# A decoder trunk on one core: the loads of the output projections spread between other projections' steps

## The chip, the core and the metric

The kernel runs on one core of one Trainium2 chip. Its time is the device time of one execution in microseconds (us); less is better. TensorE (PE) multiplies, ScalarE (ACT), VectorE (DVE) and GpSimd (POOL) do the elementwise work, SyncE (SP) issues every DMA used here.

## The reference

Two decoder layers over 1024 tokens of width 1024, and a final norm, all float32:

```python
# layer 0
z = rms_norm(x, g_in) @ w_in        # q/kv latents, rope key, sliding-window q/k/v, gate
o = concat(latent_attention(z), sliding_window_attention(z))   # 8 heads each
x = x + (o * silu(gate)) @ w_out
# layer 1
z = rms_norm(x, g_in) @ w_in        # q, k, v, forget logits, gate
o = forgetting_attention(z)         # 16 heads, causal, decay bias
x = x + (o * silu(gate)) @ w_out
out = rms_norm(x, g_final)
```

## The kernel before

Every matrix product is done in three TensorE passes on split operands: a float32 value is cast to a high part on ACT, and the low part is the difference (`split`, `split_sb`; lines 104, 105, 112, 113). `mm3` (lines 116 to 118) issues high times high, high times low and low times high.

**Attention.** A unit is one head and one half of the queries. It makes rows of logits into PSUM (lines 116 to 118 or 268, 269), DVE takes the running minimum (line 322), ACT the exponential (line 329), POOL scales the row (line 284). Then TensorE transposes the row, 128 columns at a time, into PSUM (line 355), ACT and DVE split it into `ph` and `pl` (lines 104, 105), and TensorE multiplies with the values (lines 346, 347). PSUM has two banks each for logits (`s`), transposes (`t`), values (`o`) and projections (`pj`).

**Order on TensorE.** It is written out by hand. `run_units` reads a string for each unit: T is a transpose group, L a row of logits, M a value product, F one step of other work. F calls `fill.step()`, which takes the next step of the first entry of `fill.work`, if all that this entry waits for is done. An entry is a projection that the current heads don't need yet (16 steps: 8 for each half of the tokens), or one token block of an output projection (4 steps). Each step is three or six matmuls on 512 columns. `fill.loads` is a second list, taken in order as soon as an entry is free, without counting steps. Where the work of a layer's list is left after its last unit, `fill.drain()` issues it back to back.

**Order on the other engines.** ACT, DVE, POOL and SP are ordered by a scheduler, from its own estimate of when operands are ready and a buffer is free. So a load or a cast can stand in its engine's queue well ahead of its place in the program.

**The output projections.** Layer 0's is done in two parts: `swa_out` (line 1004) for the sliding-window heads, 8 blocks for each half `q` of the output columns, with weights from `swa_wo(q)` (line 995, four pieces of 128x512 into `kx` tiles); and `out0` (line 1126) for the latent heads, with weights from `load_wo` (line 1063, eight pieces into the `hh`, `hl` tiles that held the normed input). Layer 1's is `out1_first` and `out1` (lines 1288 and 1295), with sixteen pieces from `load_wo`. A block of gated heads (`ogs`) is read back from memory into a `wr` tile and split into `wh` and `wl` at the start of the block's own first step (`swa_out`, `out_parts`). There are 5 `wr` tiles and 3 each of `wh` and `wl`; the weights of every projection pass through the same tiles.

**When the weights are loaded before.** All four pieces of `swa_wo(0)` in one entry of `fill.loads`; all four of `swa_wo(1)` at the end of block 7 of the first half; all eight pieces of layer 0's second part in one entry of `fill.loads`, after the last gate projection; eight pieces of layer 1 when the first half of gate 6 is written, and two more in each of the next four blocks.

Of the kernel before, what the change touches and what calls it, by code (L numbers as in the profile page):

```python
# [13 lines left out]
F32R = mybir.dt.float32r  # L14
# [5 lines left out]
P = 128  # L20
# [41 lines left out]
def trunk(ctx, tc, x, positions, e_g_in, e_w_in, e_g_q_a, e_w_q_up, e_g_kv_a, e_w_kv_up,  # L62
# [47 lines left out]

    def split_sb(hi, lo, raw, engine=None):
        nc.scalar.copy(out=hi, in_=raw)  # L112
        (engine or nc.gpsimd).tensor_tensor(out=lo, in0=raw, in1=hi.bitcast(F32), op=ALU.subtract)  # L113
# [310 lines left out]
    class Filler:  # L424


        def __init__(self):
            self.work, self.loads, self.done = [], [], set()

        def add(self, name, gen, after=()):  # L430
# [3 lines left out]
        def load(self, name, gen, after=()):  # L434
            self.loads.append((name, gen, after))

        def free(self, items):
            return items and all(a in self.done for a in items[0][2])

# [8 lines left out]
        def step(self):  # L448
            self.ahead()
            if self.free(self.work):  # L450
                try:
                    next(self.work[0][1])
                except StopIteration:
                    self.done.add(self.work.pop(0)[0])
                    self.step()

        def need(self, *names, ready=None):
            for name in names:
                while name not in self.done and not (ready and ready()):
                    self.ahead()  # L460
                    if name not in self.done:
                        assert self.free(self.work), (name, self.work[0], self.loads[:1])
                        self.step()

        def drain(self):
            while self.work or self.loads:
                self.ahead()
                assert self.free(self.work) or not self.work, self.work[0]
                self.step()

    fill = Filler()
# [532 lines left out]
    def swa_out(q, blk):  # L1004
# [6 lines left out]
        nc.sync.dma_start(out=r, in_=x[tok, cols])  # L1011
        acc = pst("pj")
# [10 lines left out]
    def first_wo():  # L1023
        swa_wo(0)
        yield

    units = []
# [8 lines left out]
    for h in range(8):  # L1036
        fill.load(f"prep{h}", mla_prep(h, heads[h]),
                  [[("rows", "swa", 5, 1)], [("rows", "swa", 7, 1), ("pv", "swa", 6, 1)],
                   [("rows", "mla", 0, 1), ("pv", "swa", 7, 1)]][h] if h < 3 else
                  [("rows", "mla", h - 2, 1), ("pv", "mla", h - 3, 1)])  # L1040
        if h == 1:
            fill.load("wp", first_wo(), [("rows", "swa", 7, 1)])
    for pr in range(4):
        for d, G in UNIT_ORDER[pr == 3]:
            units.append(mla_unit(2 * pr + d, G))
    for w in WORK0.split():
        kind, i = w[0], int(w[1])
        if kind == "q":
            fill.add(f"qs{i}", swa_q(i), [("rows", "swa", 2 * i - 3, 1)] * (i > 1))
        elif kind == "s":  # L1050
            fill.add(f"sgate{i}", gate_chunk(swa_gate(i), hT, None, ogs0[i]), [("pv", "swa", 2 * i + 1, 1)])
        elif kind == "p":
            q, blks = ((0, range(NB)), (1, range(4)), (1, range(4, NB)))[i]
            for blk in blks:
                fill.add(f"p{q}{blk}", swa_out(q, blk), ["wp", "sgate3", ("pv", "swa", 7, 1)])
# [7 lines left out]
    def load_wo(w, e0, halves):  # L1063

        n = KC - e0
        for nh in range(2):
            if nh * n % KC == 0:
# [10 lines left out]
    def out_parts(blk, ogs, own, e0s):  # L1078

        tok = slice(blk * P, (blk + 1) * P)  # L1080
        parts = []
        for e0 in e0s:
            raw = sbt("wr", [4, P])
            oh, ol = sbt("wh", [4, P], F32R), sbt("wl", [4, P], F32R)
            n = 4 if e0 == 0 else 3
            nc.sync.dma_start(out=raw[:, 0:n, :], in_=ogs[e0:e0 + n, :, tok].rearrange("e p t -> p e t"))
            split_sb(oh[:, 0:n, :], ol[:, 0:n, :], raw[:, 0:n, :])
            if e0:
# [3 lines left out]

    def out_proj(nh, blk, parts, wo, resid, dst=None, e0=0, part=slice(0, 512)):

# [6 lines left out]
        for e, og in enumerate(parts):  # L1101
            mm3(acc, *og, wh[:, e0 + e, part], wl[:, e0 + e, part], e == 0, e == len(parts) - 1)
            if e < len(parts) - 1:
                yield
        nc.vector.tensor_tensor(out=r if dst is None else dst, in0=acc, in1=r, op=ALU.add)
        if dst is None:
# [19 lines left out]
    def out0(nh, blk):  # L1126
        if nh == 0:
            xa.append(sbt(("qh", "ql", "kh", "kl")[blk] if blk < 4 else "r1", [D]))
        half = xa[blk][:, nh * 512:(nh + 1) * 512]
        yield from out_proj(nh, blk, out_parts(blk, ogs0, pairs[3]["ot"], [4]), wo, xps, half)  # L1130
        square_sum(half, ssqs[nh][blk // 4][:, blk % 4:blk % 4 + 1])
# [113 lines left out]
    wo1_parts = []  # L1245
    wo1_load = load_wo(wo1, 0, wo1_parts)

    def fox_gate(pr, halves=(0, 1)):
        evac = gate_evac(fox[pr]["gt"])

        def and_load(hf, acc):
            evac(hf, acc)
            if (pr, hf) == (6, 0):
                for _ in range(KC):
                    next(wo1_load)
        return project([(w1, FG + pr * P, FG + (pr + 1) * P)], hT, and_load, halves)

# [28 lines left out]
    fill.load("gfin", final_gain(), [("rows", "fox", 13, 1)])  # L1286

    def out1_first(nh, blk):
        parts = out_parts(blk, ogs1, None, [0])
        for _ in range(KC // len(FIRST)):  # L1290
            next(wo1_load, None)
        yield from out_proj(nh, blk, parts, wo1_parts, x1s)
        yield

    def out1(blk):
        y = [sbt("r0", [512]) for _ in range(2)]
        e0s = [4] if blk in FIRST else [0, 4]
        parts = out_parts(blk, ogs1, fox[7]["ot"], e0s)
        pieces = [(0, 0, 512), (1, 0, 512)] if blk < NB - 1 else [(0, 0, 512), (1, 0, 256), (1, 256, 512)]
        total = None  # L1300
        for nh, a, b in pieces:
            cols = y[nh][:, a:b]
            yield from out_proj(nh, blk, parts, wo1_parts, x1s, cols, e0s[0], slice(a, b))
            ss = sbt("sm", [1])
# [9 lines left out]
        for nh in range(2):  # L1314
# [4 lines left out]
            nc.sync.dma_start(out=out[blk * P:(blk + 1) * P, nh * 512:(nh + 1) * 512], in_=y[nh])  # L1319

    for nh in range(2):
        for blk in FIRST:
            fill.add(f"first{nh}{blk}", out1_first(nh, blk))
    for blk in range(NB):
        fill.add(f"out1{blk}", out1(blk), ["gfin", ("pv", "fox", 15, blk // 4)])
    with tc.manual_schedule(engines={mybir.EngineType.PE}):
# [23 lines left out]
```

## Time and profile before

| | us |
|---|---|
| median of 3 runs | 1194.89 (1194.58 to 1195.39) |
| the profiled execution | 1195.06 |
| its span, first to last instruction | 1193.3 |
| TensorE busy in the span | 1168.4 (98%) |
| VectorE, ScalarE, GpSimd busy | 726.3, 702.5, 594.1 |

A busy share is an average over stages; a matmul's end in the profile is modelled, so a matmul that starts late can still look back to back with the one before. A stretch of idle time in front of an instruction stands in brackets with what ended it.

### The profile page before, as it was taken

The numbers are of one execution on the slowest core, as the hardware profiler recorded it, in microseconds if no ns is written. First come the engines' busy times: TensorE is split into PE (matmuls) and PEld (weight loads), VectorE is DVE, ScalarE is ACT, GpSimd is POOL, SyncE is SP. The second block draws the span as 40 slices with busy tenths as digits, with TensorE's granted clock in tenths as the row PEclk, the third lists the DMA queues.
The fourth block names the chain that finished last, engine by engine and source line by source line (L and its number), as shares of the span: only waits on it lengthen the run. The fifth ranks groups of instructions, "written<-read, shape, count | busy, mean of one in ns | idle before, by whom it ended". The sixth has DMA issues, their size and how long they took to land. (4 is left out here: it accounts for less than half of the span.)

```text
span 1193.3 us, 20029 instructions
## 1 busy us (share of the span) xinstructions
PE 1168.4 (98%) x6600; PEld 1001.9 (84%) x6600; DVE 726.3 (61%) x1921; ACT 702.5 (59%) x1585; POOL 594.1 (50%) x741
## 2 busy tenths in 40 slices
PE   9999999999999999999999999999999999999997
PEld 6898788888888877889998888888888888877886
DVE  6673466677777776663004666666666666667754
ACT  5445477776776665555115667676767675766532
POOL 6421154565655565335005556656555555568452
PEclk9999999999999999999999999999999999999999
DMA  6326522454653452654213222313222323147441
GB/s 202 96 63 229 159 46 62 125 150 133 164 164 106 135 155 89 201 175 135 85 56 100 62 72 62 89 57 95 61 81 71 84 59 106 63 130 230 164 157 62
DMA packets 157086, 135.30 MB, mean 113 GB/s; under 512 B 53259, under 2 KB 121638, under 8 KB 156982
## 3 DMA queue, kind: packets, MB, share of 16 engines
q1 hardware_dynamic: 156982, 134.02, 37.3%
q8 instruction: 52, 0.85, 0.3%
q14 instruction: 52, 0.43, 0.1%
HBM read 96.43 MB, written 37.55 MB: 112 GB/s over the span
## 5 line engine op out<-in xcount | busy, mean ns | idle before, releaser
L116 PE MATMUL pj<-hh,wh 128*128 128x512 f32 (+1 forms) x792 | 320.3, 404 | 0.0
L118 PE MATMUL pj<-hh,wl 128*128 128x512 f32 (+1 forms) x792 | 308.8, 390 | 0.6 <-POOL wl L113 0.6
L117 PE MATMUL pj<-hl,wh 128*128 128x512 f32 (+1 forms) x792 | 308.6, 390 | 0.0
L113 POOL TENSOR_TENSOR wl<-wr,wh 128x512 fp32r<-128x512 f32 (+1 forms) x130 | 163.7, 1262 | 137.9 <-ACT wh L112 121.3
L284 POOL TENSOR_SCALAR r<-r,sm 128x256 f32<-128x256 f32 (+4 forms) x250 | 170.8, 692 | 121.4 <-DVE sm L331 68.1
L105 DVE TENSOR_TENSOR pl<-t,ph 128x512 fp32r<-128x512 f32 (+1 forms) x320 | 178.8, 564 | 84.7 <-ACT ph L104 82.5
L104 ACT CAST ph<-t 128x512 fp32r<-128x512 f32 (+1 forms) x320 | 153.8, 484 | 110.5 <-PE t L355 92.5
L118 PEld LDWEIGHTS pj<-hh,wl 128*128 128x128 f32 x792 | 148.7, 188 | 33.4 <-POOL wl L113 1.0
L329 ACT ACTIVATE r<-r,sm 128x128 f32<-128x128 f32 (+7 forms) x184 | 143.1, 778 | 55.5 <-DVE sm L322 53.6
L116 PEld LDWEIGHTS pj<-hh,wh 128*128 128x128 f32 x792 | 149.1, 188 | 22.0 <-ACT r L891 0.4
L117 PEld LDWEIGHTS pj<-hl,wh 128*128 128x128 f32 x792 | 149.5, 189 | 20.5
L355 PE MATMUL t<-ident,r 128*128 128x128 f32 x828 | 135.6, 273 | 6.4 <-DVE pl L105 4.6
L355 PEld LDWEIGHTS t<-ident,r 128*128 128x128 f32 x828 | 103.5, 140 | 34.5 <-DVE pl L105 6.0
L112 ACT CAST wh<-wr 128x512 fp32r<-128x512 f32 (+1 forms) x130 | 77.7, 599 | 54.6 <-PE pj L117 23.9
L316 POOL TENSOR_TENSOR ld<-ld,zrow 128x128 f32<-128x128 f32 x128 | 57.9, 463 | 100.2 <-DVE sm L322 78.6
L346 PE MATMUL o<-ph,v 128*128 128x512 f32 (+3 forms) x288 | 106.9, 371 | 0.0
L347 PE MATMUL o<-pl,v 128*128 128x512 f32 (+3 forms) x288 | 99.4, 346 | 0.0
L322 DVE CUSTOM_DVE_ANT_0 r<-s,ld 128x512 f32<-128x512 f32 (+1 forms) x120 | 67.6, 563 | 47.2 <-PE s L269 44.1
L293 POOL TENSOR_TENSOR v<-ge,v 128x512 fp32r<-128x512 f32 x26 | 34.6, 1331 | 91.9 <-ACT v L292 91.9
L346 PEld LDWEIGHTS o<-ph,v 128*128 128x128 f32 x288 | 54.4, 189 | 7.7
L347 PEld LDWEIGHTS o<-pl,v 128*128 128x128 f32 x288 | 54.6, 190 | 6.2
L276 DVE TENSOR_TENSOR og<-o,ob 64x512 f32<-64x512 f32 x64 | 43.9, 686 | 10.7 <-ACT ob L275 9.7
(337 smaller groups left out, 2432.7 us busy)
## 6 DMA issues: line engine op xcount, KB each, us to landing
wr<-in_o_w_in SPq DMA_DIRECT2D x62, 256.0 KB, 3.2
ld<-lcs SPq DMA_DIRECT2D x16, 512.0 KB, 3.9
ogs<-og SPq DMA_DIRECT2D x28, 256.0 KB, 2.0
wr<-ogs SPq DMA_DIRECT2D x28, 256.0 KB, 3.6
ge<-vscr SPq DMA_DIRECT2D x24, 256.0 KB, 3.2
gt<-x1s SPq DMA_DIRECT2D x23, 256.0 KB, 2.8
wr<-ogs SPq DMA_DIRECT2D x24, 192.0 KB, 3.2
wr<-in_e_w_in SPq DMA_DIRECT2D x16, 256.0 KB, 3.3
```

The source lines that it names most:

```text
L104: nc.scalar.copy(out=hi, in_=src)
L105: nc.vector.tensor_tensor(out=lo, in0=src, in1=hi.bitcast(F32), op=ALU.subtract)
L112: nc.scalar.copy(out=hi, in_=raw)
L113: (engine or nc.gpsimd).tensor_tensor(out=lo, in0=raw, in1=hi.bitcast(F32), op=ALU.subtract)
L116: nc.tensor.matmul(out=o, lhsT=ah, rhs=bh, start=first, stop=False)
L117: nc.tensor.matmul(out=o, lhsT=ah, rhs=bl, start=False, stop=False)
L118: nc.tensor.matmul(out=o, lhsT=al, rhs=bh, start=False, stop=last)
L284: nc.gpsimd.tensor_scalar(out=row, in0=row, scalar1=rc, scalar2=scale, op0=ALU.mult, op1=ALU.mult)
L329: nc.scalar.activation(out=row[:, 0:L], in_=row[:, 0:L], func=AF.Exp, scale=-1.0, bias=mn, accum_out=den)
L346: nc.tensor.matmul(out=O[0][:, cols], lhsT=v()[:, j, :], rhs=ph[:, cols], start=j == 0, stop=False)
L347: nc.tensor.matmul(out=O[0][:, cols], lhsT=v()[:, j, :], rhs=pl[:, cols], start=False, stop=j == n - 1)
L355: nc.tensor.transpose(out=t[:, b * P:(b + 1) * P], in_=rows[b][:, j * P:(j + 1) * P], identity=ident)
```

## The change

Four things are changed, and no arithmetic.

1. `Filler` gets a third list, `sides`: an entry advances by one piece at every `every`-th step of other work that is taken while the entry is free (4 for `swa_wo`, 2 for `load_wo`). `unblock` advances it at once where the first entry of `work` waits for nothing but that side entry.
2. `swa_wo` and `load_wo` give up control after each piece. The piece's DMA is issued in one advance, and its cast and subtraction in the next; the cast is held in ACT's queue behind what the program put there before it (`keep_in_program_order`).
3. The eight pieces of layer 0's second part may begin when the first half of gate 3 is written, and a block of `out0` waits only for the four pieces that it uses. Layer 1's sixteen pieces become two entries, free when the first half of gate 6 is written and after gate 7.
4. The gated heads of a block are read and split during the second step of the block before it (`more`, `out_load`, `swa_load`), where there is one in the same list.

```diff
-    def split_sb(hi, lo, raw, engine=None):
-        nc.scalar.copy(out=hi, in_=raw)
+    def split_sb(hi, lo, raw, engine=None, in_order=False):
+        cast = nc.scalar.copy(out=hi, in_=raw)
+        if in_order:
+            tc.keep_in_program_order(cast)
...
+        def side(self, name, gen, every, after=()):
+
+            self.sides.append((name, gen, after, every))
+
+        def missing(self, items):
+            return [a for a in items[0][2] if not (a() if callable(a) else a in self.done)]
...
+        def advance(self):
+
+            if next(self.sides[0][1], self) is self:
+                self.done.add(self.sides.pop(0)[0])
+
+        def unblock(self):
+
+            while self.work and self.free(self.sides):
+                rest = self.missing(self.work)
+                if not rest or any((a[0] if type(a) is tuple else a) != self.sides[0][0] for a in rest):
+                    break
+                self.advance()
...
         def step(self):
             self.ahead()
+            self.unblock()
             if self.free(self.work):
+                if self.free(self.sides):
+                    self.ticks += 1
+                    if self.ticks % self.sides[0][3] == 0:
+                        self.advance()
...
     def swa_wo(q):
+        late = None
...
-            split_sb(wh, wl, raw)
+            if late:
+                late()
+            late = partial(split_sb, wh, wl, raw, None, True)
+            yield
+        late()
+        yield
...
+    def swa_out(q, blk, more=None):
+
+        tok, cols = slice(blk * P, (blk + 1) * P), slice(512 * q, 512 * (q + 1))
+        oh, ol, r = ahead.pop(("swa", q, blk), None) or swa_load(q, blk)
         acc = pst("pj")
         for e, (wh, wl) in enumerate(swa["wo"]):
             mm3(acc, oh[:, e, :], ol[:, e, :], wh, wl, e == 0, e == 3)
             if e < 3:
                 yield
+            if e == 0 and more:
+                more()
...
-        if blk == NB - 1 and q == 0:
-            swa_wo(1)
...
+    fill.side("wp0", swa_wo(0), 4, [("rows", "swa", 7, 1)])
+    fill.side("wp1", swa_wo(1), 4, [f"p0{NB - 1}"])
...
-        if h == 1:
-            fill.load("wp", first_wo(), [("rows", "swa", 7, 1)])
...
             for e in range(n):
                 raw = sbt("wr", [512])
                 nc.sync.dma_start(out=raw, in_=w[e * P:(e + 1) * P, nh * 512:(nh + 1) * 512])
-                split_sb(wh[:, e, :], wl[:, e, :], raw, nc.vector if e % 2 else nc.gpsimd)
+                if late:
+                    late()
+                    fill.done.add((name, pieces))
+                pieces += 1
+                late = partial(split_sb, wh[:, e, :], wl[:, e, :], raw, nc.vector if e % 2 else nc.gpsimd, True)
                 yield
...
+    def out_load(blk, ogs, e0):
+
+        tok, n = slice(blk * P, (blk + 1) * P), 4 if e0 == 0 else 3
+        raw = sbt("wr", [4, P])
+        oh, ol = sbt("wh", [4, P], F32R), sbt("wl", [4, P], F32R)
+        nc.sync.dma_start(out=raw[:, 0:n, :], in_=ogs[e0:e0 + n, :, tok].rearrange("e p t -> p e t"))
+        split_sb(oh[:, 0:n, :], ol[:, 0:n, :], raw[:, 0:n, :])
+        return oh, ol
...
-    fill.load("wo0", load_wo(wo0, 4, wo), ["gate3", "sgate3"])
+    fill.side("wo0", load_wo("wo0", wo0, 4, wo), 2, [lambda: pairs[3]["gt"][0] is not None, "sgate3"])
...
-                fill.add(f"out0{nh}{blk}", out0(nh, blk), ["wo0", ("pv", "mla", 7, hf)])
+                fill.add(f"out0{nh}{blk}", out0(nh, blk), [("wo0", 4 * nh + 4), ("pv", "mla", 7, hf)])
...
-            if (pr, hf) == (6, 0):
-                for _ in range(KC):
-                    next(wo1_load)
...
-        for _ in range(KC // len(FIRST)):
-            next(wo1_load, None)
...
+    fill.side("wo1a", load_wo("wo1a", wo1, 0, wo1_parts, (0,)), 2, [lambda: fox[6]["gt"][0] is not None])
+    fill.side("wo1b", load_wo("wo1b", wo1, 0, wo1_parts, (1,)), 2, ["fgate7"])
     for nh in range(2):
         for blk in FIRST:
-            fill.add(f"first{nh}{blk}", out1_first(nh, blk))
+            fill.add(f"first{nh}{blk}", out1_first(nh, blk), [("wo1" + "ab"[nh], 4)])
```

## Rows read from the trace of the kernel before

**Rows 1.** The page: busy us, share of the span and instructions of each engine.

```profile
PE 1168.4 (98%) x6600; PEld 1001.9 (84%) x6600; DVE 726.3 (61%) x1921; ACT 702.5 (59%) x1585; POOL 594.1 (50%) x741
```

**Rows 2.** Windows: length, busy us (instructions) of each engine, granted clock, DMA, GB/s.

```profile
425.00:437.00 12.00, 10.12 (x57) 8.09 (x56) 8.80 (x15) 9.09 (x21) 8.37 (x7) 1.00 0.61 192
437.00:467.00 30.00, 27.88 (x151) 23.31 (x150) 19.88 (x53) 17.77 (x39) 16.60 (x19) 1.00 0.36 110
900.00:1000.00 100.00, 100.00 (x536) 84.24 (x535) 62.99 (x171) 66.16 (x142) 54.75 (x73) 1.00 0.25 70
1050.00:1080.00 30.00, 26.01 (x136) 20.78 (x135) 20.61 (x43) 19.64 (x45) 23.64 (x23) 1.00 0.56 172
```

**Rows 3.** Timeline of PE: start, us, instruction, [idle before, and what ended it].

```profile
342.48 0.66 PE L355 MATMUL t<-ident,r 128*128 128x128 f32 x4 [0.90 <-DVE pl L105]
...
362.12 0.45 PE L116 MATMUL s<-kh,qh 128*128 128x384 f32 x1 [0.74 <-DVE sm L322]
...
428.04 0.39 PE L346 MATMUL o<-ph,v 128*128 128x512 f32 x1
428.27 0.39 PE L347 MATMUL o<-pl,v 128*128 128x512 f32 x1
430.51 0.80 PE L355 MATMUL t<-ident,r 128*128 128x128 f32 x3 [1.85 <-DVE pl L105]
...
454.59 0.33 PE L355 MATMUL t<-ident,r 128*128 128x128 f32 x1 [1.53 <-POOL r L284]
...
1063.00 0.44 PE L355 MATMUL t<-ident,r 128*128 128x128 f32 x2 [1.46 <-DVE pl L105]
...
1066.13 0.51 PE L118 MATMUL pj<-hh,wl 128*128 128x512 f32 x1 [0.60 <-POOL wl L113]
...
1079.86 0.33 PE L355 MATMUL t<-ident,ql 128*128 128x128 f32 x1 [1.77 <-DVE pl L105]
```

**Rows 4.** Timeline of ACT, in front of and in the same gaps.

```profile
339.81 0.62 ACT L112 CAST wh<-wr 128x512 fp32r<-128x512 f32 x1 [2.48 <-DMA wr<-in_e_w_in]
...
425.64 2.69 ACT L112 CAST hh<-wr 128x512 fp32r<-128x512 f32 x5
428.24 0.96 ACT L104 CAST ph<-t 128x512 fp32r<-128x512 f32 x2
...
1060.57 0.62 ACT L112 CAST hh<-wr 128x512 fp32r<-128x512 f32 x1 [0.77 <-DMA wr<-in_o_w_out]
...
1064.09 0.62 ACT L112 CAST wh<-wr 128x512 fp32r<-128x512 f32 x1 [2.03 <-DMA wr<-in_o_w_in]
...
1074.70 2.17 ACT L112 CAST hh<-wr 128x512 fp32r<-128x512 f32 x4
```

**Rows 5.** Timelines of POOL and DVE: subtractions of weight pieces and of a head's keys.

```profile
357.07 3.53 POOL L113 TENSOR_TENSOR kx<-wr,kx 128x512 fp32r<-128x512 f32 x2
...
359.48 2.20 DVE L113 TENSOR_TENSOR kl<-ld,kh 64x1024 fp32r<-64x1024 f32 x1
...
1076.21 2.72 DVE L113 TENSOR_TENSOR hl<-wr,hh 128x512 fp32r<-128x512 f32 x2
...
1082.80 0.68 DVE L113 TENSOR_TENSOR hl<-wr,hh 128x512 fp32r<-128x512 f32 x1
```

**Rows 6.** Line 113 by engine and tile: count, ns min/median/max, first and last start.

```profile
L113 POOL TENSOR_TENSOR hl<-wr,hh x12: 1284/1296/1968, 426.3 to 1087.1; 128x512 fp32r<-128x512 f32 x12
...
L113 DVE TENSOR_TENSOR hl<-wr,hh x12: 677/1246/1780, 426.8 to 1087.2; 128x512 fp32r<-128x512 f32 x12
...
L113 DVE TENSOR_TENSOR kl<-ld,kh x8: 1207/1225/2252, 137.2 to 414.6; 64x1024 fp32r<-64x1024 f32 x6, 128x1024 fp32r<-128x1024 f32 x2
```

**Rows 7.** Groups by line: matmuls of `swa_out`, busy us, mean ns, idle before.

```profile
L116 PE MATMUL pj<-kx,wh 128*128 128x512 f32 x64 | 26.6, 415 | 0.0
```

**Rows 8.** Timeline of SP around 1040 us, and a transfer of the chain.

```profile
1039.00 8.56 SPq L1074 DMA_DIRECT2D wr<-in_o_w_out  x3
...
1058.64 5.37 DMA wr<-in_o_w_in
```

More of the change, by code (lines that the diff above doesn't have):

```diff
@@ L428, in __init__ @@
             self.work, self.loads, self.done = [], [], set()
+            self.sides, self.ticks = [], 0
         def add(self, name, gen, after=()):
@@ L435, in load @@
             self.loads.append((name, gen, after))
+        def side(self, name, gen, every, after=()):
+            self.sides.append((name, gen, after, every))
+        def missing(self, items):
+            return [a for a in items[0][2] if not (a() if callable(a) else a in self.done)]
         def free(self, items):
-            return items and all(a in self.done for a in items[0][2])
+            return items and not self.missing(items)
+        def advance(self):
[7 more added lines that the diff above has]
+                self.advance()
         def ahead(self):
@@ L461, in need @@
                     if name not in self.done:
+                        self.unblock()
                         assert self.free(self.work), (name, self.work[0], self.loads[:1])
@@ L467, in drain @@
                 self.ahead()
+                self.unblock()
                 assert self.free(self.work) or not self.work, self.work[0]
                 self.step()
+            while self.sides:
+                self.advance()
     fill = Filler()
@@ L1001, in swa_wo, with swa_load @@
                 nc.sync.dma_start(out=raw[at], in_=wo0[row + 64 * e:row + 64 * e + 64, 512 * q:512 * (q + 1)])
-            split_sb(wh, wl, raw)
-    def swa_out(q, blk):
+            if late:
[4 more added lines that the diff above has]
+        yield
+    ahead = {}
+    def swa_load(q, blk):
         tok, cols = slice(blk * P, (blk + 1) * P), slice(512 * q, 512 * (q + 1))
@@ L1011, in swa_out @@
         nc.sync.dma_start(out=r, in_=x[tok, cols])
+        return oh, ol, r
+    def swa_out(q, blk, more=None):
+        tok, cols = slice(blk * P, (blk + 1) * P), slice(512 * q, 512 * (q + 1))
+        oh, ol, r = ahead.pop(("swa", q, blk), None) or swa_load(q, blk)
         acc = pst("pj")
@@ L1016, in swa_out @@
                 yield
+            if e == 0 and more:
+                more()
         nc.vector.tensor_tensor(out=r, in0=acc, in1=r, op=ALU.add)
         nc.sync.dma_start(out=xps[tok, cols], in_=r)
-        if blk == NB - 1 and q == 0:
-            swa_wo(1)
         yield
-    def first_wo():
-        swa_wo(0)
-        yield
+    fill.side("wp0", swa_wo(0), 4, [("rows", "swa", 7, 1)])
+    fill.side("wp1", swa_wo(1), 4, [f"p0{NB - 1}"])
     units = []
@@ L1054, in trunk, with more @@
             for blk in blks:
-                fill.add(f"p{q}{blk}", swa_out(q, blk), ["wp", "sgate3", ("pv", "swa", 7, 1)])
+                def more(q=q, blk=blk + 1, last=blk == blks[-1], i=i):
+                    if not last:
+                        ahead["swa", q, blk] = swa_load(q, blk)
+                    elif i == 2 and ("pv", "mla", 5, 1) in fill.done:
+                        ahead[0, 0] = out_load(0, ogs0, 4)
+                fill.add(f"p{q}{blk}", swa_out(q, blk, more), [f"wp{q}", "sgate3", ("pv", "swa", 7, 1)])
         else:
@@ L1060, in trunk, with load_wo @@
                      [("pv", "mla", 2 * i - 3, 1)] * (i > 1))
-    def load_wo(w, e0, halves):
-        n = KC - e0
-        for nh in range(2):
+    def load_wo(name, w, e0, halves, nhs=(0, 1)):
+        n, pieces, late = KC - e0, 0, None
+        for nh in nhs:
             if nh * n % KC == 0:
@@ L1074, in load_wo, with out_parts @@
                 nc.sync.dma_start(out=raw, in_=w[e * P:(e + 1) * P, nh * 512:(nh + 1) * 512])
-                split_sb(wh[:, e, :], wl[:, e, :], raw, nc.vector if e % 2 else nc.gpsimd)
-                yield
-    def out_parts(blk, ogs, own, e0s):
-        tok = slice(blk * P, (blk + 1) * P)
+                if late:
[3 more added lines that the diff above has]
+                late = partial(split_sb, wh[:, e, :], wl[:, e, :], raw, nc.vector if e % 2 else nc.gpsimd, True)
+                yield
+        late()
+        fill.done.add((name, pieces))
+        yield
+    def out_load(blk, ogs, e0):
[5 more added lines that the diff above has]
+        return oh, ol
+    def out_parts(blk, ogs, own, e0s, loaded=None):
         parts = []
         for e0 in e0s:
[L1083 to L1087, printed above, removed]
+            oh, ol = loaded or out_load(blk, ogs, e0)
+            loaded = None
             if e0:
@@ L1091, in out_parts, with out_proj @@
         return parts
-    def out_proj(nh, blk, parts, wo, resid, dst=None, e0=0, part=slice(0, 512)):
+    def out_proj(nh, blk, parts, wo, resid, dst=None, e0=0, part=slice(0, 512), more=None):
         n = part.stop - part.start
@@ L1104, in out_proj @@
                 yield
+            if e == 0 and more:
+                more()
         nc.vector.tensor_tensor(out=r if dst is None else dst, in0=acc, in1=r, op=ALU.add)
@@ L1129, in out0, with more @@
         half = xa[blk][:, nh * 512:(nh + 1) * 512]
-        yield from out_proj(nh, blk, out_parts(blk, ogs0, pairs[3]["ot"], [4]), wo, xps, half)
+        parts = out_parts(blk, ogs0, pairs[3]["ot"], [4], ahead.pop((nh, blk), None))
+        follow = OUT0[OUT0.index((nh, blk)) + 1:][:1]
+        def more():
+            for n, b in follow:
+                ahead[n, b] = out_load(b, ogs0, 4)
+        yield from out_proj(nh, blk, parts, wo, xps, half, more=more)
         square_sum(half, ssqs[nh][blk // 4][:, blk % 4:blk % 4 + 1])
@@ L1135, in out0 @@
         yield
-    fill.load("wo0", load_wo(wo0, 4, wo), ["gate3", "sgate3"])
+    fill.side("wo0", load_wo("wo0", wo0, 4, wo), 2, [lambda: pairs[3]["gt"][0] is not None, "sgate3"])
+    OUT0 = [(nh, 4 * hf + b) for hf in range(2) for nh in range(2) for b in range(4)]
     for hf in range(2):
@@ L1245, in trunk @@
     wo1_parts = []
-    wo1_load = load_wo(wo1, 0, wo1_parts)
     def fox_gate(pr, halves=(0, 1)):
-        evac = gate_evac(fox[pr]["gt"])
-        def and_load(hf, acc):
-            evac(hf, acc)
-            if (pr, hf) == (6, 0):
-                for _ in range(KC):
-                    next(wo1_load)
-        return project([(w1, FG + pr * P, FG + (pr + 1) * P)], hT, and_load, halves)
+        return project([(w1, FG + pr * P, FG + (pr + 1) * P)], hT, gate_evac(fox[pr]["gt"]), halves)
     units = []
@@ L1286, in trunk, with load_ahead @@
     fill.load("gfin", final_gain(), [("rows", "fox", 13, 1)])
+    OUT1 = [(nh, blk) for nh in range(2) for blk in FIRST] + [(None, blk) for blk in range(NB)]
+    def load_ahead(*follow):
+        for n, b in follow:
+            if n is not None or ("pv", "fox", 13, 1) in fill.done:
+                ahead[n, b] = out_load(b, ogs1, 4 if n is None and b in FIRST else 0)
     def out1_first(nh, blk):
-        parts = out_parts(blk, ogs1, None, [0])
-        for _ in range(KC // len(FIRST)):
-            next(wo1_load, None)
-        yield from out_proj(nh, blk, parts, wo1_parts, x1s)
+        parts = out_parts(blk, ogs1, None, [0], ahead.pop((nh, blk), None))
+        follow = OUT1[OUT1.index((nh, blk)) + 1:][:1]
+        more = partial(load_ahead, *follow)
+        yield from out_proj(nh, blk, parts, wo1_parts, x1s, more=more)
         yield
@@ L1297, in out1 @@
         e0s = [4] if blk in FIRST else [0, 4]
-        parts = out_parts(blk, ogs1, fox[7]["ot"], e0s)
+        parts = out_parts(blk, ogs1, fox[7]["ot"], e0s, ahead.pop((None, blk), None))
+        follow = OUT1[OUT1.index((None, blk)) + 1:][:1]
         pieces = [(0, 0, 512), (1, 0, 512)] if blk < NB - 1 else [(0, 0, 512), (1, 0, 256), (1, 256, 512)]
@@ L1302, in out1 @@
             cols = y[nh][:, a:b]
-            yield from out_proj(nh, blk, parts, wo1_parts, x1s, cols, e0s[0], slice(a, b))
+            yield from out_proj(nh, blk, parts, wo1_parts, x1s, cols, e0s[0], slice(a, b),
+                                more=partial(load_ahead, *follow) if (nh, a) == (0, 0) else None)
             ss = sbt("sm", [1])
```

2 lines of the change are left out of this document (1 added, 1 removed).

## Prediction

> **What bounds the kernel.** First the page's table of engines. TensorE is busy 98% of the span and every other engine under 62% [rows 1], so only time in which TensorE starts late, or fewer matmuls, can pay. The change takes no matmul away. So I went through the windows, to see where TensorE isn't full. From 900 to 1000 us it has no idle time at all, with DVE at 63% and ACT at 66%. From 425 to 437 it lacks 1.88 of 12 us, from 437 to 467 it lacks 2.12 of 30, from 1050 to 1080 it lacks 3.99 of 30 [rows 2]. In just these places the weights of the output projections are split. Third, the timeline of TensorE gives the gaps one by one, with who ended each: seven of 0.5 us or more between 300 and 1100 us that I could tie to one cause [rows 3]. Last, the timelines of the engines that ended them say why they were late.
>
> The reader is to see the same picture three times on ACT. At 425.64 five casts of weight pieces stand together, 2.69 us, and the two casts of transposes that TensorE waits for come after them, at 428.24. At 1074.70 four stand together, 2.17 us. At 1060.57 one cast waits 0.77 us for its transfer, with others behind it [rows 4]. DVE shows the sequel: two subtractions of pieces take 2.72 us from 1076.21, and TensorE idles 1.77 us until the difference behind them is made [rows 3, 5]. Each burst begins when a tile of the normed input comes free: the scheduler had all loads of pieces early and let all casts go as soon as they could.
>
> **What the six gaps cost.** In brackets stand 0.90, 0.74, 1.85, 1.46, 0.60 and 1.77 us, together 7.32 (the seventh, 1.53 at 454.59, belongs to a row's scaling on POOL and is not counted) [rows 3]. The bracket is less than the loss, since the matmul before ends late in the profile. At 428.27 the next matmul would start 0.23 us later, as the one before shows, and starts 2.24 us later: 2.01 lost where the bracket has 1.85. With 0.16 more for each of six, the loss is 8.3 us.
>
> **The change part by part.**
>
> *Pieces one by one, casts held in order* (parts 1 to 3). Nothing is added or taken away: the same 8 pieces of `swa_wo` and 24 of `load_wo`, each one transfer (two for `swa_wo`), one cast of 0.62 us, and one subtraction, on POOL 1.30 us or on DVE, for every second piece of `load_wo`, 1.25 us in the median and 0.68 alone [rows 4 to 6]. What moves is where they stand. Counting the steps F of the list, layer 0's second eight get one piece for two steps from about 427 to 457 us; layer 1's first eight from about 1053 to 1075, one in 2.7 us where five stood in 2.69; its second eight from 1077 to some 1092. The second half of `swa_wo` moves from the end of block 7 into the 24 steps of gates 1 and 2. By gap:
>
> - 342.48 (0.90): ACT sits 2.48 us for the transfer of a gate's weights [rows 4]. The four pieces of `swa_wo(1)` hold four of the five `wr` tiles, as they wait for `kx` tiles that block 7 still reads, so the gate's load is issued late. After the change the gate's two loads come before most pieces. Gone.
> - 362.12 (0.74): DVE's minimum stands behind the subtraction of a head's keys, 2.20 us while POOL subtracts two pieces in 3.53 [rows 5]; the shortest one of this shape takes 1.21 [rows 6]. The pieces move some 8 us away. Gone.
> - 430.51, 1063.00, 1079.86 (1.85, 1.46, 1.77): the bursts. Gone as bursts.
> - 1066.13 (0.60): gate 7's weights, whose transfer took 5.37 us from 1058.64 [rows 8]; all eight pieces of layer 1's first half were issued ahead of it. Now four are. Gone, I take it.
>
> What is late next: the pieces land between casts and differences that have no slack marked. The gap at 1079.86 gives a measure: 2.72 us of subtractions in front cost 1.77 [rows 3, 5], so about 0.95 us in front costs nothing. A median subtraction on DVE of 1.25 us then costs 0.30; twelve of them 3.6 us, if each stands straight in front of a difference that TensorE needs; none, if each runs in 0.68. The row at 1082.80, one piece alone in 0.68 us with no gap on TensorE behind it, speaks for the low end [rows 5]. I take 2.1, a little over half, because a cast of 0.62 us on ACT now and then does the same and isn't in that sum.
>
> How long a subtraction takes beside POOL is the least known term. The rows show 0.68 alone, 1.25 in the median and 1.78 at most [rows 6]. The Trainium skill, SBUF — State Buffer, section "Who interferes with whom", states that a DVE instruction with two SBUF inputs and a GpSimd instruction that reads SBUF exclude each other for the whole instruction, so the second is fully blocked. The trace agrees where both engines subtract together: 2.20 us against 1.21 for the keys [rows 5, 6]. By that rule spreading would not help a piece that meets one of POOL's scalings; it is a rival below.
>
> *Gated heads one block ahead* (part 4). The same 52 loads (counted from the loops), casts and subtractions, placed three steps earlier in the program. Worth nothing: the 64 first matmuls of the blocks of `swa_out` had 0.0 us idle in front of them [rows 7], because the scheduler had these loads far ahead already. If that cover were gone, a block would cost up to 5.37 us for a slow transfer, 0.62 and 1.30, that is 7.3 us [rows 4, 6, 8]; the move makes it less likely, not more. From 467 us on, and at the end, TensorE runs back to back; there nothing can be won.
>
> *SP's queue.* As many DMAs as before, in another order. A piece's raw tile is now held until the next advance, so an instruction of SP that waits for a free `wr` tile holds up what stands behind it: weights of gates, blocks of heads, a head's bias, stores. Before, this is seen at 1039.00, where three issues of pieces take 8.56 us in all [rows 8]. I cost it at nothing: the first four or five pieces are held as long before.
>
> **Sum.** 8.3 won, 2.1 given back, 0 for the heads: 6.2 us. The profiled execution took 1195.06 us, 1.8 of them outside the span, and 0.17 more than the median of 1194.89; from the median it is 1188.7 us. Bounds: nothing given back and the POOL gap closed too (1.53 + 0.16) makes 10.0 less, 1184.9; all 3.6 given back, 1190.2.
>
> **Rivals.**
>
> *Given back* (within 0.2%, which is 2.4 us and about what a measurement of this kernel can tell from no change). If DVE and POOL exclude each other, each of the twelve subtractions on DVE meets one of POOL's and takes 1.78 us; less the slack of 0.95 that is 0.83, times twelve 10.0 us lost against 8.3 won: 1196.6. The Trainium skill's rule above would have it so. Half of them meeting makes 1191.6 and ten 1194.9. For it: POOL is busy 55% where nothing else is wrong [rows 2]. Against it: POOL's scalings are shorter than its subtractions, and the single piece above met none. 0.19.
>
> *Weights late* (slower). The place is the five `wr` tiles in the two gates after each burst. A held piece keeps a tile for one or two steps more; if the loads of gate weights go behind it in SP's queue, TensorE stands for up to 5.37 + 0.62 + 1.30 = 7.3 us at a projection's first step. It decides from 10.7 us lost, so from two such projections, uncovered: 1194.9 - 8.3 + 14.6 = 1201. For it: the 0.60 and the 0.90 in the brackets are this wait already, in small [rows 3]. Against it: they came when eight and four pieces stood ahead, now there are fewer. 0.12.
>
> *More than the gaps* (over 9 us less). Hidden delays under 0.1 us in the same stretches and the gap at 454.59 go too: up to 1184.9. It needs pieces to leave the stretch of 437 to 467 us, but four come in. 0.07.
>
> **How the numbers follow.** The forecast, 3 to 9 us less, has 0.62 and its own range is 1186 to 1192. With the rival above it, faster by over 0.2% has 0.69; same 0.19; slower 0.12. The range runs from 1184.8, the lower bound, to 1196, which leaves out the slower case and a part of the unchanged one.
>
> **What would show it.** Right: no group of more than two casts of pieces on ACT between 420 and 1100 us; brackets at the six places gone or under 0.3 us; TensorE's idle time from 425 to 437 under 0.5 us and from 1050 to 1080 under 1.5; a median under 0.9 us for pieces on DVE. Wrong: new brackets in front of transposes between 437 and 467 or 1053 and 1092 us, ended by DVE, with a piece just ahead (the port); or in front of a projection's first step, ended by POOL's difference of `wh` (late weights). What I can't see is how the scheduler orders everything else once these casts are held; it could open gaps where there were none, and that would make the prediction wrong without any of its steps being so.

## The result, and the profile after

The changed kernel took 1204.06 us in the median of four runs (1203.73 to 1205.57), against 1195.14 us (1194.58 to 1195.91) for the kernel before on the same chip: ratio 1.0076, 95% interval 1.0062 to 1.0090. So it is slower by some 9 us, outside the predicted range. The profiled execution has a span of 1202.5 us, 9.2 more than before.

Against [rows 1] the page has the same 6600 matmuls, 2.8 us more busy time of TensorE, and 6.4 us more in which it is idle. The groups of the page say what it waits for, behind the bar: the high part `wh` on ACT and the low part `wl` on POOL. Of these waits the kernel before had 0.60 us [rows 3].

```profile
PE 1171.2 (97%) x6600; PEld 1003.6 (83%) x6600; DVE 723.4 (60%) x1921; ACT 702.9 (58%) x1585; POOL 590.6 (49%) x741
...
L118 PE MATMUL pj<-hh,wh 128*128 128x512 f32 (+1 forms) x792 | 321.1, 405 | 4.2 <-ACT wh L112 3.8
L120 PE MATMUL pj<-hh,wl 128*128 128x512 f32 (+1 forms) x792 | 309.5, 391 | 2.4 <-POOL wl L115 2.4
...
L118 PE MATMUL pj<-kx,wh 128*128 128x512 f32 x64 | 27.1, 424 | 0.0
```

The windows of [rows 2], and one more behind them, of the changed kernel:

```profile
425.00:437.00 12.00, 10.90 (x60) 9.02 (x59) 7.89 (x21) 8.90 (x21) 8.60 (x8) 1.00 0.47 141
437.00:467.00 30.00, 25.03 (x119) 20.35 (x118) 16.31 (x41) 15.09 (x32) 15.92 (x16) 0.89 0.39 122
900.00:1000.00 100.00, 100.00 (x539) 84.53 (x538) 63.83 (x174) 66.89 (x143) 55.77 (x77) 1.00 0.24 68
1050.00:1080.00 30.00, 27.95 (x145) 22.69 (x144) 14.32 (x39) 16.80 (x40) 16.16 (x20) 1.00 0.37 110
1080.00:1105.00 25.00, 19.59 (x85) 14.46 (x84) 16.46 (x32) 13.47 (x27) 18.82 (x17) 0.93 0.74 232
```

Where the bursts of casts stood, TensorE is fuller: idle 1.10 instead of 1.88 us from 425 to 437, and 2.05 instead of 3.99 from 1050 to 1080, 2.7 us won. Right behind it loses more: 4.97 instead of 2.12 us idle from 437 to 467, and 5.41 us from 1080 to 1105, where before it had none; 8.3 us lost. In both of these windows the granted clock is below 1.00, too. Another 1.9 us of idle time came in from 500 to 600 us (99.51 us busy before, 97.56 after), where no piece is loaded.

Windows at fixed times hold different work in the two kernels. Both traces have their 6600 matmuls in the same order, so each can be set beside its partner: the one at 430.51 [rows 3], for instance, starts at 423.88 in the changed kernel. By start times before, the changed kernel is behind by:

| at, us | 53 | 341 | 428 | 470 | 600 | 1050 | 1100 |
|---|---|---|---|---|---|---|---|
| behind, us (minus: ahead) | -2.5 | -3.6 | -4.6 | 0.8 | 2.6 | 2.7 | 8.9 |

The first 2.5 us come before anything of the change has begun; 1.6 of them are a fall of the clock that only the trace of the kernel before has there (last section).

The timeline of TensorE gives the gaps of the changed kernel, with who ended each. Most are new; the matmul at 453.78 had 1.53 us in front of it before, at 454.59 [rows 3], and the one at 443.77 had 0.48.

```profile
364.49 0.66 PE L357 MATMUL t<-ident,r 128*128 128x128 f32 x4 [0.91 <-DVE pl L105]
...
433.14 0.50 PE L120 MATMUL pj<-kx,wl 128*128 128x512 f32 x1 [1.10 <-POOL wl L115]
...
443.77 0.50 PE L118 MATMUL s<-kh,qh 128*128 128x512 f32 x1 [2.14 <-DVE sm L324]
...
453.78 0.33 PE L357 MATMUL t<-ident,r 128*128 128x128 f32 x1 [1.99 <-POOL r L286]
...
1067.08 0.50 PE L118 MATMUL pj<-hh,wh 128*128 128x512 f32 x1 [1.38 <-ACT wh L112]
1068.44 0.50 PE L120 MATMUL pj<-hh,wl 128*128 128x512 f32 x1 [0.63 <-POOL wl L115]
1082.32 0.44 PE L270 MATMUL s<-kh,qh 128*128 128x384 f32 x1 [0.88 <-DVE sm L324]
...
1094.10 0.50 PE L118 MATMUL pj<-hh,wh 128*128 128x512 f32 x1 [1.11 <-ACT wh L112]
1095.98 0.50 PE L120 MATMUL pj<-hh,wl 128*128 128x512 f32 x1 [1.15 <-POOL wl L115]
1101.16 0.50 PE L118 MATMUL pj<-hh,wh 128*128 128x512 f32 x1 [1.35 <-ACT wh L112]
```

The gap of 2.14 us at 443.77 names DVE, but most of it is made earlier, on ACT and in SP's queue. Follow the next three fences, the timelines of SP, ACT and DVE, backwards from it:

```profile
433.26 1.98 SPq L1122 DMA_DIRECT2D wr<-in_e_w_out  x3
436.52 1.63 SPq L1048 DMA_DIRECT2D wr<-ogs  x2
```

```profile
439.98 0.62 ACT L112 CAST wh<-wr 128x512 fp32r<-128x512 f32 x1 [2.95 <-DMA wr<-ogs]
440.50 0.58 ACT L104 CAST ph<-t 128x512 fp32r<-128x512 f32 x1
441.52 0.62 ACT L112 CAST wh<-wr 128x512 fp32r<-128x512 f32 x1 [0.44 <-DMA wr<-ogs]
442.05 0.47 ACT L104 CAST ph<-t 128x384 fp32r<-128x384 f32 x1
...
1085.74 0.62 ACT L112 CAST wh<-wr 128x512 fp32r<-128x512 f32 x1 [1.83 <-DMA wr<-ogs]
...
1100.49 0.62 ACT L112 CAST wh<-wr 128x512 fp32r<-128x512 f32 x1 [3.15 <-DMA wr<-ogs]
```

```profile
441.12 0.69 DVE L105 TENSOR_TENSOR pl<-t,ph 128x512 fp32r<-128x512 f32 x1 [0.72 <-ACT ph L104]
442.56 0.56 DVE L105 TENSOR_TENSOR pl<-t,ph 128x384 fp32r<-128x384 f32 x1 [0.75 <-ACT ph L104]
443.03 0.68 DVE L324 CUSTOM_DVE_ANT_0 r<-s,zrow 128x512 f32<-128x512 f32 x1
```

SP issues three pieces of weights, and only then, at 436.52, two blocks of gated heads (`ogs`). ACT's queue has the cast of these heads ahead of two casts of transposes, and stands 2.95 us for the transfer. DVE's differences and minimum come behind the casts, and TensorE behind the minimum. The two last rows of ACT are the same wait in layer 1; behind the one at 1100.49 stands TensorE's gap at 1101.16.

In layer 1 it is the same, in SP's timeline. Gate 7's weights are issued at 1062.57 (1058.64 before [rows 8]), and the first block of gated heads at 1070.23 (1060.22 before).

```profile
1041.65 8.56 SPq L1122 DMA_DIRECT2D wr<-in_o_w_out  x3
...
1062.57 1.05 SPq L155 DMA_DIRECT2D wr<-in_o_w_in  x2
1066.43 2.97 SPq L1122 DMA_DIRECT2D wr<-in_o_w_out  x3
1070.23 0.38 SPq L1138 DMA_DIRECT2D wr<-ogs  x1
```

What SP waited for says what held the heads. From 380 to 470 us it stood with an issue of gated heads in front (lines 1048 and 1138) until the subtraction of a piece (`hl`) was done, which frees the piece's raw tile: 20.1 us in the three largest rows. The last row is the only such wait there in the kernel before, 1.2 us. A row gives the total in us, how often, and the longest:

```profile
SPq L1138 <- DVE hl L115: 9.8, 2, 6.7
SPq L1048 <- POOL hl L115: 6.8, 2, 6.0
SPq L1048 <- DVE hl L115: 3.5, 1, 3.5
...
SPq L1008 <- POOL hl L113: 1.2, 2, 1.0
```

So the theory before the experiments, **Theory A**: the first pieces are transferred as early as before (387 to 409 us for layer 0, from 1041.65 on for layer 1), but their casts are now held at their place in the program, and until then each keeps one of the five `wr` tiles. What else goes through `wr` comes late. Rivals: **B**, the gated heads a block ahead cost the time themselves; **C**, the casts and subtractions cost by the places in ACT's, POOL's and DVE's queues to which the change moves them, whatever tiles they use.

### The profile page after: what moved, and what is told of

It reads as the page before. It is cut to its first block, busy times and chain, and to the rows that moved or that the text cites. A ratio compares the mean times of both kernels' runs of the same rounds, so it can differ in the third digit from the quotient of the medians.

```text
span 1202.5 us, 20009 instructions
## 1 busy us (share of the span) xinstructions
PE 1171.2 (97%) x6600; PEld 1003.6 (83%) x6600; DVE 723.4 (60%) x1921; ACT 702.9 (58%) x1585; POOL 590.6 (49%) x741
## 5 line engine op out<-in xcount | busy, mean ns | idle before, releaser
L333 DVE RECIPROCAL sm<-sm 128x1 f32<-128x1 f32 x192 | 30.8, 161 | 35.6 <-ACT r L331 30.8
```

## The experiments

All ratios are to the kernel before, on the same chip as the run beside it. A sixth raw tile takes 2 KB a partition; to make room, the count of small `sm` tiles goes from 32 to 24 where `wr` and `wx` together have six.

**Without the loads a block ahead, and with them alone.** Rival B, from both sides. The first kernel drops the calls of `more` in the changed kernel; the second puts the weights back as they were before and keeps `more`.

```diff
                 def more(q=q, blk=blk + 1, last=blk == blks[-1], i=i):
+                    return
...
-            for n, b in follow:
+            for n, b in ():
```

> The new loading of the weights, with the gated heads loaded by the block that uses them, as before. Theory A (pieces that wait for their held cast keep the five raw `wr` tiles, so the gated heads and a gate's weights are loaded late, and PE stops for them): the pieces are issued as in the changed kernel, so the loss stays: 1201 to 1206 us, with waits of PE's first products of a block on ACT's and POOL's split near 431, 1092 and 1099 us. Theory B (the gated heads that are loaded a block ahead cost the time themselves, by taking raw tiles and places in ACT's queue earlier): most of the loss goes: 1187 to 1195 us.

> The kernel before with the gated heads loaded a block ahead, and the weights of the projections loaded as before. The loads stand in the same order on every queue as in the kernel before, so both theories expect no change: ratio 0.998 to 1.002. If loads a block ahead gain or cost by themselves, the ratio lies outside.

Without them: 1206.53 us, ratio 1.0067 (1.0051 to 1.0083); them alone: 1.0002 (0.9989 to 1.0015). B falls: the loss is there without the loads ahead, and alone they cost nothing that this measurement can tell.

**The hold taken away.**

```diff
-            late = partial(split_sb, wh, wl, raw, None, True)
+            late = partial(split_sb, wh, wl, raw, None, False)
...
-                late = partial(..., nc.vector if e % 2 else nc.gpsimd, True)
+                late = partial(..., nc.vector if e % 2 else nc.gpsimd, False)
```

> The casts of the pieces are not held behind what ACT's queue had before them. Theory A: a piece's cast may follow its transfer at once and gives its `wr` tile back, so the gated heads come as early as before and the long waits on them go; but the casts bunch in ACT's queue again, as in the kernel before: 1193 to 1198 us. Theory C (casts and subtractions at these places in the stream cost the time): 1200 to 1206 us.

1193.9 us, ratio 0.9965 (0.9951 to 0.9979): the whole loss goes, and the kernel is some 4 us faster than the one before. Its windows:

```profile
425.00:437.00 12.00, 10.12 (x56) 7.88 (x54) 7.98 (x13) 8.41 (x20) 7.95 (x7) 1.00 0.58 171
437.00:467.00 30.00, 27.35 (x148) 22.78 (x148) 19.90 (x54) 17.99 (x40) 16.74 (x18) 1.00 0.39 119
1050.00:1080.00 30.00, 28.43 (x149) 23.30 (x148) 18.36 (x43) 20.01 (x46) 22.43 (x23) 1.00 0.57 169
1080.00:1105.00 25.00, 25.00 (x131) 21.08 (x131) 18.05 (x48) 15.67 (x33) 20.02 (x20) 1.00 0.78 241
```

The loss from 1080 to 1105 is gone, that from 437 to 467 is down to 0.5 us, the clock is whole, and the gain from 1050 to 1080 has stayed; from 425 to 437 TensorE is as idle as before. The casts do bunch again, as expected (five in 2.69 us from 1054.59, as in [rows 4]), so bursts cost less here than the hold that was to undo them.

**The hold in one layer at a time.**

```diff
-                late = partial(..., nc.vector if e % 2 else nc.gpsimd, True)
+                late = partial(..., nc.vector if e % 2 else nc.gpsimd, name == "wo0")
```

The other kernel has `name != "wo0"` there, and `False` in `swa_wo`.

> The changed kernel with the casts held only for the pieces of layer 0 (`wp` and `wo0`), not for `wo1`. By Theory A the loss lies where the held pieces meet the gated heads; the stretch 425 to 475 us lost 4.1 us to the kernel without any hold, the stretch 1075 to 1125 us lost 8.7. So this kernel is 4 us over the one without holds: ratio to the kernel before 0.998 to 1.002. If a hold costs at one place alone because of the order of the whole stream, it is as fast as without (0.9965) or as slow as the changed kernel (1.0076).

> The changed kernel with the casts held only for the pieces of `wo1`. By Theory A, with the same working, it is 8 to 9 us over the kernel without holds: ratio to the kernel before 1.002 to 1.006, with the waits of PE on the gated heads' split near 1092 and 1099 us and none near 431 us. By the rival, 0.9965 or 1.0076.

Layer 0 held: 1.0001 (0.9991 to 1.0010). Layer 1 held: 1.0035 (1.0022 to 1.0048). Both as worked out: 0.36% and 0.70% over the kernel without holds, together 1.06%, where the changed kernel lies 1.11% over it. Each brings its own layer's gaps back. TensorE in the kernel that holds layer 0:

```profile
433.67 0.49 PE L120 MATMUL pj<-kx,wl 128*128 128x512 f32 x1 [1.10 <-POOL wl L115]
...
444.34 0.50 PE L118 MATMUL s<-kh,qh 128*128 128x512 f32 x1 [2.18 <-DVE sm L324]
...
452.98 0.47 PE L357 MATMUL t<-ident,r 128*128 128x128 f32 x1 [2.00 <-POOL r L286]
```

and in the kernel that holds layer 1:

```profile
1088.38 0.50 PE L118 MATMUL pj<-hh,wh 128*128 128x512 f32 x1 [1.25 <-ACT wh L112]
1090.13 0.79 PE L120 MATMUL pj<-hh,wl 128*128 128x512 f32 x1 [1.02 <-POOL wl L115]
1095.19 0.51 PE L118 MATMUL pj<-hh,wh 128*128 128x512 f32 x1 [1.00 <-ACT wh L112]
```

**The hold kept, more raw tiles.** This parts A from C: the casts stay held, and only the tiles differ. First two tiles of their own for the pieces, four for the rest; then six shared ones.

```diff
-            "wr": (5, 2048), "wh": (3, 2048), ...
+            "wr": (4, 2048), "wx": (2, 2048), "wh": (3, 2048), ...
...
-                raw = sbt("wr", [512])
+                raw = sbt("wx", [512])
```

```diff
-            "wr": (5, 2048), "wh": (3, 2048), ...
+            "wr": (6, 2048), "wh": (3, 2048), ...
```

> The pieces get two raw tiles of their own and `wr` keeps four, six in all instead of five; order of casts and transfers as in the changed kernel. Theory A: the gated heads no longer wait behind a piece, but have one tile less among themselves: 1191 to 1199 us, and the waits of PE on the gated heads' split near 431 and 1092 to 1101 us go. Theory C: as in the changed kernel, 1201 to 1206 us.

> The changed kernel, casts held, with six `wr` tiles for all instead of five. Theory A (the held pieces keep raw tiles from the gated heads): a sixth tile lets one more head through and gives back a part, 2 to 7 us of 9: ratio to the kernel before 1.001 to 1.006. Rival (the hold costs by its place in ACT's queue alone): 1.0065 to 1.009.

Own tiles: 1196.7 us, ratio 0.9988 (0.9974 to 1.0001). Six shared: 1193.3 us, ratio 0.9969 (0.9955 to 0.9983), more than A gave it. One raw tile turns 0.76% slower into 0.31% faster, with every cast still held. With own tiles TensorE has no wait on `wh` or `wl` left, but it stands 5.7 us for rows that POOL scales, 1.8 before: for this part C may be right. The control, the kernel before with six tiles:

> The kernel before with six `wr` tiles. The transfers of the weights of the output projections wait there for raw tiles too (five of them took 15.67 us to be issued from 1041.93 us on). If that wait costs something, 0.995 to 0.999; if not, 0.999 to 1.001; if a sixth tile only lets casts bunch, 1.001 to 1.005.

1.0003 (0.9991 to 1.0015): there the sixth tile is worth nothing that can be told, so in the changed kernel it cures something that the change did.

The waits of these kernels, in one table (us in total; in the first column of waits ACT stands for a transfer of gated heads, in the second TensorE stands for `wh` or `wl`):

| kernel | ratio | ACT for `ogs` | PE for `wh`, `wl` |
|---|---|---|---|
| before | 1 | 0.3 | 0.6 |
| changed | 1.0076 | 11.4 | 7.3 |
| without the loads ahead | 1.0067 | 14.3 | 10.3 |
| layer 1 held | 1.0035 | 8.8 | 5.1 |
| layer 0 held | 1.0001 | 6.3 | 1.1 |
| own two tiles | 0.9988 | 0.3 | 0 |
| six tiles, held | 0.9969 | 11.0 | 0.2 |
| no hold | 0.9965 | 3.0 | 0 |

TensorE's wait falls with the ratio, but for one row and a step of 0.2 us. ACT's own wait doesn't: with six tiles it still stands 11.0 us for the heads, and TensorE hardly waits for their split any more, 0.2 us. So how long ACT stands doesn't settle it; that it matters which use a late head meets is my reading and isn't shown.

**One raw tile for the pieces.** As above, with `wx` of one buffer beside five `wr`, and each piece's cast ahead of the next one's transfer.

```diff
+                if late:
+                    late()
+                    fill.done.add((name, pieces))
                 raw = sbt("wx", [512])
                 nc.sync.dma_start(out=raw, in_=w[...])
-                if late:
-                    late()
-                    fill.done.add((name, pieces))
```

> The pieces get one raw tile of their own (`wx`), and a piece's cast is put ahead of the next piece's transfer; the five `wr` tiles serve the gated heads, the gates' weights and the values alone. Theory A (held raw tiles): the waits on the gated heads near 431 and 1092 to 1101 us and the half clock behind them go, so about 8 us of the 9 lost come back: 1190 to 1197 us. Theory C (the held casts and the subtractions spread over POOL and DVE delay the rows of logits, whatever tile the piece lies in): no more than 2 us come back: 1201 to 1205 us.

1219.4 us, ratio 1.0176 (1.0158 to 1.0195): both expectations missed. The heads do come in time, but now the pieces are late. A piece's transfer starts when the piece before has been cast and subtracted, and at the end the products wait for the pieces themselves. SP, ACT and TensorE:

```profile
1100.83 17.24 SPq L1125 DMA_DIRECT2D wx<-in_o_w_out  x5
```

```profile
1099.46 0.62 ACT L112 CAST hh<-wx 128x512 fp32r<-128x512 f32 x1 [4.64 <-DMA wx<-in_o_w_out]
1103.35 0.62 ACT L112 CAST hh<-wx 128x512 fp32r<-128x512 f32 x1 [3.27 <-DMA wx<-in_o_w_out]
```

```profile
1104.02 0.79 PE L118 MATMUL pj<-hh,wh 128*128 128x512 f32 x1 [11.62 <-ACT hh L112]
```

So the early transfers that held the tiles were also what covered the pieces' latency: some 4 us a piece, one after another.

**No hold, with other tiles, and without the loads ahead.**

> No casts held, and the pieces in two raw tiles of their own beside four `wr` tiles. Theory A (the hold hurts through the raw tiles it keeps): without the hold there is nothing left for own tiles to cure, so the ratio stays at 0.995 to 0.999, as without the hold alone. Theory C (the places of casts in the queues): own tiles shift the casts again, and the ratio moves by more than 0.003 in either direction.

> No hold, and six shared `wr` tiles. If raw tiles still limit when the hold is gone, it is faster yet: 0.992 to 0.996. If the five tiles are what spreads the pieces' casts (as six tiles, two of them the pieces' own, gave 1.0033), the casts bunch again: 0.998 to 1.004.

> No hold, and the gated heads loaded by the block that uses them. If what the kernel without holds wins (0.9965) comes from the pieces given between steps, it keeps it: 0.995 to 0.9985. If it comes from the heads a block ahead, it is lost: 0.9985 to 1.0015.

Own tiles without the hold: 1.0033 (1.0020 to 1.0046). A expected no change from 0.9965 and missed; here C is right that places count: TensorE doesn't wait for `wh` or `wl` at all, and ACT doesn't for heads. The loss lies in layer 1: from 1050 to 1105 TensorE idles 8.8 us, with five shared tiles 1.6. POOL subtracts a piece in 1.72 us at 1076.00 right ahead of a scaling, and TensorE idles 3.00 us for that row at 1078.12; it is the longest gap, but not the whole loss. Six shared tiles without the hold: 1189.21 us, ratio 0.9934 (0.9920 to 0.9947), as the first expectation for it said, faster than both kernels and the best of the study. Without the hold and the loads ahead: 0.9987 (0.9977 to 0.9998), just inside the band for "lost"; its interval reaches into the other band and touches that of the kernel with them, so whether these loads win 0.2% beside the pieces is open.

Side by side, hold against raw tiles:

| | five `wr` tiles | six |
|---|---|---|
| casts held | 1.0076 | 0.9969 |
| not held | 0.9965 | 0.9934 |

The hold costs 1.1% with five tiles and still 0.35% with six, and the two intervals with six don't meet. So one more raw tile takes away about two thirds of its cost; whether a seventh takes more, no run shows. With six tiles the mean granted clock of the executions is 0.9946 with the hold and 0.9980 without. The difference, 0.0034 of 1190 us, is 4.0 us, about as much as the 4.1 us between the two kernels, but that the clock is the cause isn't shown.

## Why the prediction was wrong

**The step that failed** is the one on SP's queue: "I cost it at nothing: the first four or five pieces are held as long before." They aren't. Before, a piece's cast went as soon as its place was free, five in 2.69 us, and gave five tiles back at once; held, the first five casts of layer 0 are spread from 424.80 to 434.00 us and the first of layer 1 start at 1060.52 instead of 1052.98. The steps counted in the prediction put layer 1's casts at 1053 to 1075 and 1077 to 1092; they came at 1060.5 to 1079.2 and 1088.3 to 1101.0, of which only 2.7 us are the lag that the kernel had by then. In the same text the queue was seen to hold up "weights of gates, blocks of heads", and no price was put on it. It measured 7.3 us of TensorE's waits on `wh` and `wl`, which made the matmuls behind them 8.6 us later against their partners; 1.7 us that came in at 443.77, behind ACT's wait of 2.95 us; and 4.2 us at half clock, for which the prediction had no term.

**The cover named for the gated heads** was the scheduler, which "had these loads far ahead already". That holds while `wr` tiles are free, and part 4 alone is indeed worth nothing (1.0002). The error was to price it apart from parts 1 to 3, which took the tiles.

**The bursts** went as said: no more than two casts of pieces stand together, and DVE's median for a piece fell from 1.246 us [rows 6] to 0.910, just short of the 0.9 that was to show it. TensorE's wait on differences of transposes (`pl`) fell from 6.4 to 0.9 us. Of the 8.3 us won on paper nearly all came: set beside their partners, the matmuls at 342.48, 362.12, 430.51, 1063.00 and 1079.86 have no gap left, and those behind them gained 1.1, 1.0, 2.3, 1.7 and 2.0 us, together 8.1. The fixed windows show only 2.7 of it, because the new delays fall into the same windows and between them. Soon after 362.12 another gap came (0.91 at 364.49, a difference for which DVE stood 1.99 us behind a gate's output on ACT); 1066.13 was "gone, I take it" and grew from 0.60 to 1.38 and 0.63.

**The 2.1 us given back** came once in twelve on DVE: it subtracts a piece in 1.75 us at 1079.85, and TensorE idles 0.88 us at 1082.32 for the minimum behind it. The rival "Given back" had 0.83 for such a meeting, so its mechanism and its price are right in this case, but it needed twelve. The pieces on POOL, which the sum left out, do it too: POOL subtracts one in 1.26 us at 451.38, right ahead of the row that TensorE awaits at 453.78.

**The rival "Weights late"** had the right place, the five `wr` tiles, the right sign and 1201 us (1204 measured), with 0.12. It looked for the wait in gates' weights, of which one case came (2.0 us, at 1067.08 and 1068.44). Most of it were the gated heads, which have the same queue and tiles. What was to show it, a projection's first step that waits for POOL's difference of `wh`, came at 433.14, 1068.44 and 1095.98.

**The reordering that I couldn't see** is real, as the last paragraph of the prediction feared: 0.68% lies between two kernels without holds that differ only in tiles. The 1.9 us from 500 to 600 us belong here too, but not to the hold: the kernel with part 4 alone also has 97.56 us busy there.

## What to carry to other kernels

A load that is issued early and used late costs its buffer for all the time between: count what else passes through that pool, and price a moved cast by what its tile keeps out. When casts are to be spread late, give the pool one more buffer: here one tile of 2 KB a partition was worth 1.1% with the hold, 0.3% without it and nothing before the change. Fewer buffers for the spread load don't replace it: with a single one the pieces themselves came late, 1.8% slower than before. And a wait for a transfer in ACT's queue is paid by what is queued behind it: read the chain back over the engines before believing the name in the bracket. Where the matmuls keep their order, compare partners and not windows of time.

## What the runs showed of the hardware

The granted clock fell to half in the changed kernel three times while TensorE worked, shortly after it had come back from idle time. Stretches inside the falls, the first with what stands ahead of it, and three matmuls on 512 columns from the second row:

```profile
443.77:445.38 1.61, 1.61 (x8) 1.43 (x9) 1.54 (x5) 1.17 (x3) 0.80 (x1) 0.89 0.83 257
445.38:448.30 2.92, 2.92 (x9) 2.34 (x8) 1.59 (x7) 1.54 (x4) 0.90 (x1) 0.50 0.12 35
...
455.40:458.50 3.10, 3.10 (x11) 2.51 (x10) 2.03 (x4) 1.10 (x2) 1.00 (x1) 0.50 0.41 132
...
1097.00:1099.20 2.20, 2.20 (x7) 1.65 (x5) 1.15 (x2) 0.34 (x1) 0.96 (x2) 0.50 0.80 223
```

```profile
445.98 0.63 PE L349 MATMUL o<-pl,v 128*128 128x512 f32 x1
446.41 0.63 PE L118 MATMUL s<-kh,qh 128*128 128x512 f32 x1
446.84 0.63 PE L119 MATMUL s<-kl,qh 128*128 128x512 f32 x1
```

They start 0.43 us apart, where they start 0.23 apart at the full level of 2.4 GHz (428.04 and 428.27 in [rows 3]): the level is 1.2 GHz. Before the falls TensorE had idled 2.14 us (443.77), 0.50 and 1.99 (451.46, 453.78), and 1.11 and 1.15 (1094.10, 1095.98). In these rows at 0.50 it worked 8.2 us, so 4.1 us were lost that stand nowhere as idle time. Not all of it is the change's, for the kernel before fell to half once too, where it worked:

```profile
37.40:40.60 3.20, 3.20 (x15) 3.19 (x15) 1.37 (x4) 1.85 (x5) 2.16 (x2) 0.50 0.66 182
```

That cost it 1.6 us, so in these two traces the falls make 2.5 us of the 9.2; the page has 2.8 us more busy time for the same matmuls. It fell behind gaps of 0.78 and 0.48 us (35.50, 36.38). The changed kernel has the same two gaps at 34.66 and 35.53, and its clock stayed whole: one trace of each kernel can be off by such a fall. Over all executions the lower clock stays: 0.993 to 0.995 in the mean of each of the four of the changed kernel, and 0.997 on average in the 76 of the kernel before beside the experiments.

The Trainium skill, TensorE: Matmul & The Clock Gate, section "Wait — 56ns, not 53.3ns?", gives 426.7 ns from start to start at this level for 512 columns; the trace agrees. The same section gives 215.7 ns at the full level; the trace has 0.23 us, which is what counts here. How long one idle stretch is doesn't decide by itself in these rows: in the kernel that holds layer 0, the 2.18 us at 444.34 brought no fall, and the 2.00 at 452.98 did. The gap at 443.77 so cost 2.14 us and then about 1.5 more.
